# Attention with both heads in one instruction, and the queries' two parts stacked by transfers

## The chip, the cores and the metric

The kernel runs on one NeuronCore of a Trainium2 chip. The metric is the device time of one execution, in microseconds (us), taken over several runs. The core has five engines that run their own instruction streams in order: TensorE (PE; its weight loads are shown as PEld), VectorE (DVE), ScalarE (ACT), GpSimd (POOL) and SyncE (SP), which here only issues transfers. ACT issues some transfers too. Matmul results land in PSUM, which has eight banks of 512 fp32 values per partition; everything else is in SBUF or in the device memory.

## The reference, cut to what matters

One inference step of a two-layer decoder for 512 prompt positions and 8 sample positions, model width 1024. Layer 0 uses sliding-window attention (16 query heads, 2 key/value heads of width 64, window 128, one learned sink per head), layer 1 gated linear attention; each is followed by a gated convolutional FFN. The change is in layer 0's attention over the prompt:

```python
def sink_softmax(scores, mask, sink):
    s = jnp.where(mask, scores, NEG_INF)
    m = jnp.maximum(jnp.max(s, -1, keepdims=True), sink)
    p = jnp.exp(s - m)
    return p / (jnp.sum(p, -1, keepdims=True) + jnp.exp(sink - m))

def swa_prompt(x, w_qkv, b_qkv, sinks, w_o):
    q, k, v = qkv_proj(x, w_qkv, b_qkv, 0)          # with rotary positions
    ...                                             # blocks of 128, each with the block before it
    scores = jnp.einsum('bnqkgd,bnskd->bnkgqs', qb, kk) * ATTN_SCALE
    mask = (kpos >= 0) & (kpos <= qpos) & (qpos - kpos < WINDOW)
    probs = sink_softmax(scores, mask, sink)
    o = jnp.einsum('bnkgqs,bnskd->bnqkgd', probs, vv)
    return o @ w_o, ...
```

## The kernel before

**Units and groups.** The weights are cut into units of 128 output columns. The 520 positions are two groups: `a` has 256 prompt positions, `b` has 256 prompt and 8 sample positions. Each unit's function runs once for each group. Attention has ten units: one for the keys (`attn_k`), one for the values (`attn_v`) and eight for the queries (`attn_q`, c = 0 to 7); with two groups that is sixteen runs of `attn_q`. Unit c holds the query heads c and c + 8, one for each key/value head, stacked on partitions 0 to 63 and 64 to 127. "Both heads" below are these two, v = 0 and v = 1.

**Split numbers.** Products are made with rounded fp32 operands (fp32r). To keep fp32 accuracy each operand is a high part (a rounded copy) and a low part (the rest): `wh` and `wl` for weights (lines 156 to 161), `xh` and `xl` for activations; a product (lines 173 to 175) is three matmuls for each of eight blocks. For the scores, a query's high part is on 64 partitions and its low part on the other 64, so that one matmul with the stacked tile `qs` against `khi` and one against `klo` make all needed terms (lines 440 and 441).

**One run of `attn_q`** goes through four steps, with the next unit's product between them: (1) the product, its bias and scale on ACT (`ra`, line 362), the rotation (`rope`: a shuffle into `rb` on DVE, line 364; multiplications on POOL, line 365, and DVE, line 366; the sum `rr` on POOL, line 368), and the parts `qs` (ACT copy on line 414, DVE subtraction on line 415, once for each head, as the two heads' rows go to different partitions); (2) the scores into the PSUM tiles `sc`, one bank for each head, and for each head the masks (lines 450, 451 for group a, line 453 for group b), the sink as one more column (454), the negated maximum into `small` (455), two exponentials with their sums on ACT (457), the reciprocals (458) and the scaling of `pr` (POOL on line 463 for the first head, DVE on line 460 for the second); (3) transposes (469), a copy (471) and two triangular selections `pl` and `pu` on POOL (475); (4) the products with the values (488) and the split of the result into `hh`/`hl` or `hs` (198, 199).

**Buffers.** `sc` has two buffers in a PSUM pool that layer norm, the samples' attention and the gated linear attention use too; `tp` and `pv` have one bank each, the products four (`accp`). In SBUF `ra`, `rb`, `rr` and `qs` have two buffers each, `pr` four; the values before their transposition have one tile of their own, `vt` (line 393, read by the transposes on lines 397 and 402 and by a transfer on line 400).

**Order.** Tile's planner orders each engine's instructions along a simulated timeline, from the order in which the program makes them; buffers' releases and all semaphores come from it. Two functions of the program, `spawn` and `due`, put a unit's later steps behind the products that follow.

Of the kernel before, what the change touches and what calls it, by code (L numbers as in the profile page):

```python
# [20 lines left out]
P = 128  # L21
# [4 lines left out]
NT = SEQ + NS  # L26
# [42 lines left out]
C_SINK = C_LNB + 4 * KD  # L69
# [14 lines left out]
class Group:  # L84
    def __init__(self, i):
        self.i = i
        self.n = 256 if i == 0 else 256 + NS
        self.c0 = 256 * i
        self.name = "ab"[i]


class Net:
    def __init__(self, tc, ctx, I, O):
        self.tc, self.nc, self.I, self.O = tc, tc.nc, I, O
        self.groups = [Group(0), Group(1)]
# [12 lines left out]
        self.par = c.tile([P, NPAR], F32, name="par")  # L108
        self.ident = c.tile([P, P], F32, name="ident")
        self.ones_a = c.tile([P, P], F32, name="ones_a")  # L110
        nc.gpsimd.memset(self.ones_a, 1.0 / D)
        self.eps = c.tile([P, 2], F32, name="eps")
        nc.gpsimd.memset(self.eps[:, 0:1], NORM_EPS)
        nc.gpsimd.memset(self.eps[:, 1:2], 1.0)
        for i, g in enumerate(self.groups):
            s = [P, KD, g.n]
            g.x = self.act.tile(s, F32, name=f"x_{g.name}")


# [12 lines left out]
            g.hl = self.act.tile(s, F32R, name=f"hl_{g.name}")  # L132
        self.units = []
        self.w = {}

# [253 lines left out]
    def attn_v(self, g, u):  # L389
        nc, n = self.nc, g.n  # L390
        ps = self.product(g, u, g.xh, g.xl)
        vt = self.ap.tile([P, NT - 256], F32, name="vt", bufs=1)[:, :n]
        nc.scalar.activation(vt, ps, AF.Identity, bias=self.par[:, C_BQKV + 1:C_BQKV + 2])
        yield 1
        mp = self.mtile("tp")
        for b in range(2):
            nc.tensor.transpose(mp[:, b * P:(b + 1) * P], vt[:, b * P:(b + 1) * P], self.ident)
        nc.vector.tensor_copy(self.vtok[:, 2 * g.i:2 * g.i + 2, :], mp[:, :256].rearrange("p (b f) -> p b f", b=2))
        if g.i:
            nc.scalar.dma_start(out=self.O["v_prompt"], in_=vt[:, 128:256])  # L400
            mp = self.mtile("tp")
            nc.tensor.transpose(mp[:NS, :P], vt[:, 256:], self.ident)
            self.vs = self.ap.tile([NS, P], F32, name="vs")
            nc.vector.tensor_copy(self.vs, mp[:NS, :P])

    def attn_q(self, g, u, c):
        nc = self.nc
        ps = self.product(g, u, g.xh, g.xl)
        r = self.rope(g, ps, 0.125, self.bq[:, c:c + 1])
        qs = self.ap.tile([P, 2, 256], F32R, name="qs", bufs=2)  # L410
        for v in range(2):
            own = slice(64 * v, 64 * v + 64)
            oth = slice(64 - 64 * v, 128 - 64 * v)
            nc.scalar.activation(qs[own, v], r[own, :256], AF.Copy)
            nc.vector.tensor_tensor(qs[oth, v], r[own, :256], qs[own, v].bitcast(F32), op=ALU.subtract)  # L415
            if g.i:
# [14 lines left out]


        parts = []
        scs = [self.mtile("sc").rearrange("p (b k) -> p b k", b=2) for v in range(2)]
        for v in range(2):
            for b in range(2):
                n = 2 * g.i + b
                keys = slice(0, 256) if n == 0 else slice(P * (n - 1), P * (n + 1))
                qb = qs[:, v, b * P:(b + 1) * P]
                nc.tensor.matmul(scs[v][:, b], qb, self.khi[v][:, keys], start=True, stop=False)  # L440
                nc.tensor.matmul(scs[v][:, b], qb, self.klo[v][:, keys], start=False, stop=True)
        prs = []
        for v in range(2):
            h = c + 8 * v
            sc = scs[v]
            pr = self.ap.tile([P, 2, P + 2], F32, name="pr", bufs=4)
            small = self.ap.tile([P, 4], F32, name="small", bufs=4)
            nm, den = small[:, 0:2], small[:, 2:4]
            if g.i == 0:
                nc.vector.copy_predicated(sc[:, 0, 0:P], self.mask0.bitcast(I32), self.mask0)  # L450
                nc.vector.copy_predicated(sc[:, 1, 0:P], self.own[:, 0], sc[:, 1, P:])
            else:
                nc.vector.copy_predicated(sc[:, :, 0:P], self.own, sc[:, :, P:])
            nc.vector.tensor_copy(sc[:, :, P], self.par[:, C_SINK + h:C_SINK + h + 1].broadcast_to([P, 2]))
            nc.vector.tensor_reduce(nm, sc[:, :, 0:P + 1], axis=AX.X, op=ALU.max, negate=True)
            for b in range(2):
                nc.scalar.activation(pr[:, b, 0:P + 1], sc[:, b, 0:P + 1], AF.Exp, bias=nm[:, b:b + 1], accum_out=den[:, b:b + 1])
            nc.vector.reciprocal(den, den)
            if v:
                nc.vector.tensor_tensor(pr[:, :, 0:P], pr[:, :, 0:P], den.unsqueeze(2).broadcast_to([P, 2, P]), op=ALU.mult)  # L460
            else:
                for b in range(2):
                    nc.gpsimd.tensor_scalar(pr[:, b, 0:P], pr[:, b, 0:P], den[:, b:b + 1], 1.0, op0=ALU.mult, op1=ALU.mult)
            prs.append(pr)
        yield 1
        for pr in prs:
            tp = self.mtile("tp")[:, :256]
# [14 lines left out]
        for b in range(2):  # L482
            n = 2 * g.i + b
# [614 lines left out]
```

## Time and profile before

| | |
|---|---|
| median of 3 runs | 1159.49 us (1157.88 to 1160.13) |
| profiled execution | 1154.76 us |
| its span in the profile | 1153.0 us |
| mean granted TensorE clock | 0.992 |
| busy over the span | PE 96%, PEld 91%, DVE 70%, ACT 49%, POOL 30% |
| attention over the prompt | about the first 150 us |

The profile is of one execution. The span runs from its first to its last instruction; the time of the execution is 1.8 us longer. "Busy" is the time in which an engine has at least one instruction under way. Matmuls are pipelined, so a busy PE need not be at its peak. A row of the groups names the line, the engine, the operation, output and inputs, and then the busy time in us and the mean duration of one in ns, and the idle time of the engine just before them with what ended it. `<-` between two instructions in the list of waits reads "waited for".

### The profile page before, as it was taken

Reading aid. Unit: us, or ns where it says so; the run is one execution under the profiler, and the core shown is the slowest. Engines: PE = TensorE matmul, PEld = TensorE weight load, DVE = VectorE, ACT = ScalarE, POOL = GpSimd, SP = SyncE. Lnnn points to the kernel's source line nnn. Section 1 sums busy time; section 2 is a strip of 40 time slices with the busy share of each in tenths; the row PEclk is TensorE's granted clock in tenths of the full one; section 3 lists DMA queues with packets and bytes.
Section 4 is the critical chain, followed back from the end, with each engine's and each line's share of the span. In section 5 each row is a group of like instructions: output and inputs, shape, how many; then the busy total and the mean of one; then the engine's idle time right before and its main releaser. Section 6 shows DMA issues by size and latency. Waiting matters only on the chain.

```text
span 1153.0 us, 22833 instructions
## 1 busy us (share of the span) xinstructions
PE 1102.3 (96%) x8806; PEld 1052.4 (91%) x8806; DVE 809.6 (70%) x1679; ACT 565.2 (49%) x1228; POOL 348.0 (30%) x597
## 2 busy tenths in 40 slices
PE   7889988999999999999899999999999999999995
PEld 6788888999999999998899999898999999999994
DVE  7988869755665556568877688799756665566666
ACT  4466646633554245445545555457533553245433
POOL 5677768310011001056500100378100110010344
PEclk9999989999999999999999999999999999999998
DMA  6322022223232332243124454442323323233222
GB/s 221 129 78 88 2 76 97 83 83 119 102 109 93 97 106 92 92 132 110 38 92 126 132 185 145 153 136 68 110 91 115 106 92 110 92 103 100 74 63 75
DMA packets 48669, 118.62 MB, mean 103 GB/s; under 512 B 5768, under 2 KB 22192, under 8 KB 48560
## 3 DMA queue, kind: packets, MB, share of 16 engines
q1 hardware_dynamic: 46544, 115.41, 31.0%
q10 hardware_dynamic: 2016, 1.75, 0.5%
q8 instruction: 69, 1.13, 0.4%
q14 instruction: 40, 0.33, 0.1%
HBM read 108.67 MB, written 8.47 MB: 102 GB/s over the span
## 4 chain that ended last, share of the span: by engine, by line
PE 74%; DVE 14%; POOL 4%; issue 3%; DMA 2%; ACT 2%; SPq 0%; ACTq 0%; DVEq 0%; POOLq 0%
PE accp L174 15%; PE accp L191 15%; PE accp L175 15%; PE accp L173 15%; PE accp L192 8%; DVE wl L161 2%; DMA vb<-dv 1%; POOL x_b L298 1%; DVE qs L415 1%; POOL x_a L298 1%; DVE u L296 1%; PE pv L488 1%; DVE msq L276 1%; PE sc L761 1%; DVE rb L366 1%
## 5 line engine op out<-in xcount | busy, mean ns | idle before, releaser
L161 DVE TENSOR_TENSOR wl<-raw,wh 128x1024 fp32r<-128x1024 f32 (+2 forms) x189 | 230.5, 1221 | 107.4 <-ACT wh L158 103.3
L158 ACT ACTIVATE wh<-raw 128x1024 fp32r<-128x1024 f32 (+1 forms) x176 | 183.0, 1040 | 209.4 <-PE accp L174 196.9
L173 PE MATMUL accp<-xh_b,wh 128*128 128x264 f32 x976 | 271.6, 279 | 2.4 <-DVE hprod L594 2.4
L174 PE MATMUL accp<-xl_b,wh 128*128 128x264 f32 x976 | 271.3, 278 | 0.2
L175 PE MATMUL accp<-xh_b,wl 128*128 128x264 f32 x976 | 270.6, 277 | 0.0
L191 PE MATMUL accp<-xs_a,wh 128*128 128x512 f32 x576 | 196.3, 382 | 0.0
L173 PEld LDWEIGHTS accp<-xh_b,wh 128*128 128x128 f32 x976 | 184.9, 190 | 3.3 <-DVE hprod L594 2.8
L174 PEld LDWEIGHTS accp<-xl_b,wh 128*128 128x128 f32 x976 | 184.8, 189 | 3.1 <-DVE xl_b L301 0.6
L175 PEld LDWEIGHTS accp<-xh_b,wl 128*128 128x128 f32 x976 | 184.7, 189 | 0.6 <-issue 0.4
L192 PE MATMUL accp<-xs_a,wl 128*128 128x256 f32 x576 | 145.4, 273 | 0.0
L173 PE MATMUL accp<-hh_b,wh 128*128 128x264 f32 x480 | 134.2, 280 | 3.2 <-ACT hh_b L198 3.2
L174 PE MATMUL accp<-hl_b,wh 128*128 128x264 f32 x480 | 134.5, 280 | 0.0
L175 PE MATMUL accp<-hh_b,wl 128*128 128x264 f32 x480 | 133.6, 278 | 0.0
L191 PEld LDWEIGHTS accp<-xs_a,wh 128*128 128x128 f32 x576 | 109.2, 190 | 11.3
L173 PE MATMUL accp<-xs_a,wh 128*128 128x256 f32 x400 | 111.4, 284 | 5.7 <-DVE x_b L219 2.1
L174 PE MATMUL accp<-xs_a,wh 128*128 128x256 f32 x400 | 111.4, 281 | 3.4 <-DVE xs_a L301 2.7
L175 PE MATMUL accp<-xs_a,wl 128*128 128x256 f32 x400 | 111.1, 280 | 3.0 <-DVE wl L161 3.0
L192 PEld LDWEIGHTS accp<-xs_a,wl 128*128 128x128 f32 x576 | 110.3, 191 | 1.9
L173 PEld LDWEIGHTS accp<-hh_b,wh 128*128 128x128 f32 x480 | 91.7, 191 | 3.6 <-ACT hh_b L198 3.5
L202 POOL COPY hist<-aext 128x2 f32<-128x2 f32 x44 | 8.9, 202 | 284.7 <-DVE aext L572 281.6
L174 PEld LDWEIGHTS accp<-hl_b,wh 128*128 128x128 f32 x480 | 91.6, 191 | 1.4 <-issue 0.3
L175 PEld LDWEIGHTS accp<-hh_b,wl 128*128 128x128 f32 x480 | 91.5, 191 | 0.2
(320 smaller groups left out, 2522.1 us busy)
## 6 DMA issues: line engine op xcount, KB each, us to landing
raw<-in_w_up SPq DMA_DIRECT2D x88, 512.0 KB, 3.4
raw<-in_w_down SPq DMA_DIRECT2D x32, 512.0 KB, 3.4
raw<-in_w_gla SPq DMA_DIRECT2D x24, 512.0 KB, 3.4
raw<-in_w_mix_o SPq DMA_DIRECT2D x16, 512.0 KB, 3.5
raw<-in_w_down SPq DMA_DIRECT2D x16, 384.0 KB, 2.9
sgla<-in_state_gla SPq DMA_DIRECT2D x16, 256.0 KB, 3.1
vb<-dv SPq DMA_DIRECT2D x16, 256.0 KB, 4.0
out_gla_s<-sgla SPq DMA_DIRECT2D x16, 256.0 KB, 2.7
```

The costliest lines, as they stand in the source:

```text
L158: nc.scalar.activation(h[:, c], r[:, c], AF.Copy)
L161: nc.vector.tensor_tensor(l[:, c], r[:, c], h[:, c].bitcast(F32), op=ALU.subtract)
L173: nc.tensor.matmul(o, h[:, ks], xh, start=k == 0, stop=False)
L174: nc.tensor.matmul(o, h[:, ks], xl, start=False, stop=False)
L175: nc.tensor.matmul(o, l[:, ks], xh, start=False, stop=k == nt - 1)
L191: both = lambda: nc.tensor.matmul(o, h[:, ks], in_turn(rs[:, k].rearrange("p t q j -> p t (q j)")), start=k == 0, stop=last)
L192: low = lambda: nc.tensor.matmul(o[:, :P], l[:, ks], in_turn(rh[:, k]), start=False, stop=False)
L276: nc.vector.scalar_tensor_tensor(q, q, 0.5, nv, op0=ALU.mult, op1=ALU.mult)
L296: nc.vector.tensor_tensor(u, x[:, m], r, op=ALU.mult)
L298: ts = nc.gpsimd.tensor_scalar(x[:, m], u, sc(m), bi(m), op0=ALU.mult, op1=ALU.add)
L366: nc.vector.tensor_tensor(b, b, tab[:, 1], op=ALU.mult)
L415: nc.vector.tensor_tensor(qs[oth, v], r[own, :256], qs[own, v].bitcast(F32), op=ALU.subtract)
```

## The change

It does five things, all in layer 0's attention over the prompt but the second:

- **Parts of the queries.** The high part of both heads is made by one ACT copy and the low part by one DVE subtraction, both on 128 partitions, into a new tile `hl` (two buffers). Four transfers, issued by ACT, then put the four blocks of 64 partitions and 256 columns in their places in `qs`.
- **`sc` is one tile** of two banks for the whole program. `attn_q` uses both halves; every other user gets one half, in turn.
- **Masks, sinks, maxima, reciprocals.** One instruction works on both heads' banks where there was one for each head. Masks and sinks come from broadcast access patterns. The exponentials stay four, one for each head and block.
- **Scaling.** The scaling of both heads comes behind the reciprocals of both.
- **`vt` becomes a buffer of the tag `ra`**, which has two.

```diff
+        self.sc2, self.sc_i = self.mps.tile([P, 2, 512], F32, name="sc"), 0
...
     def mtile(self, tag):
-        return self.mps.tile([P, 512], F32, name=tag, bufs=2 if tag == "sc" else 1)
+        if tag == "sc":
+            self.sc_i += 1
+            return self.sc2[:, self.sc_i % 2]
+        return self.mps.tile([P, 512], F32, name=tag)
...
-        vt = self.ap.tile([P, NT - 256], F32, name="vt", bufs=1)[:, :n]
+        vt = self.ap.tile([P, NT - 256], F32, name="ra", bufs=2)[:, :n]
...
+        hl = self.ap.tile([P, 2, 256], F32R, name="hl", bufs=2)
+        nc.scalar.activation(hl[:, 0], r[:, :256], AF.Copy)
+        nc.vector.tensor_tensor(hl[:, 1], r[:, :256], hl[:, 0].bitcast(F32), op=ALU.subtract)
         qs = self.ap.tile([P, 2, 256], F32R, name="qs", bufs=2)
-        for v in range(2):
-            own = slice(64 * v, 64 * v + 64)
-            oth = slice(64 - 64 * v, 128 - 64 * v)
-            nc.scalar.activation(qs[own, v], r[own, :256], AF.Copy)
-            nc.vector.tensor_tensor(qs[oth, v], r[own, :256], qs[own, v].bitcast(F32), op=ALU.subtract)
+        for part in range(2):
+            for v in range(2):
+                nc.scalar.dma_start(out=qs[64 * part:64 * part + 64, v].bitcast(F32),
+                                    in_=hl[64 * v:64 * v + 64, part].bitcast(F32))
...
-        scs = [self.mtile("sc").rearrange("p (b k) -> p b k", b=2) for v in range(2)]
+        sc = self.sc2.rearrange("p v (b k) -> p v b k", b=2)
...
+        small = self.ap.tile([P, 2, 4], F32, name="small", bufs=4)
+        nm, den = small[:, :, 0:2], small[:, :, 2:4]
+        if g.i == 0:
+            nc.vector.copy_predicated(sc[:, :, 0, 0:P], self.mask0.bitcast(I32).unsqueeze(1).broadcast_to([P, 2, P]),
+                                      self.mask0.unsqueeze(1).broadcast_to([P, 2, P]))
+            nc.vector.copy_predicated(sc[:, :, 1, 0:P], self.own, sc[:, :, 1, P:])
+        else:
+            own = self.own[:, 0:1].unsqueeze(1).broadcast_to([P, 2, 2, P])
+            nc.vector.copy_predicated(sc[:, :, :, 0:P], own, sc[:, :, :, P:])
+        sink = self.par[:, C_SINK + c:C_SINK + c + 9:8]
+        nc.vector.tensor_copy(sc[:, :, :, P], sink.unsqueeze(2).broadcast_to([P, 2, 2]))
+        nc.vector.tensor_reduce(nm, sc[:, :, :, 0:P + 1], axis=AX.X, op=ALU.max, negate=True)
         for v in range(2):
...
             for b in range(2):
+                nc.scalar.activation(pr[:, b, 0:P + 1], sc[:, v, b, 0:P + 1], AF.Exp, bias=nm[:, v, b:b + 1], accum_out=den[:, v, b:b + 1])
             prs.append(pr)
+        nc.vector.reciprocal(den, den)
+        for b in range(2):
+            nc.gpsimd.tensor_scalar(prs[0][:, b, 0:P], prs[0][:, b, 0:P], den[:, 0, b:b + 1], 1.0, op0=ALU.mult, op1=ALU.mult)
+        nc.vector.tensor_tensor(prs[1][:, :, 0:P], prs[1][:, :, 0:P], den[:, 1].unsqueeze(2).broadcast_to([P, 2, P]), op=ALU.mult)
```

More of the change, by code (lines that the diff above doesn't have):

```diff
@@ L409, in attn_q @@
         r = self.rope(g, ps, 0.125, self.bq[:, c:c + 1])
+        hl = self.ap.tile([P, 2, 256], F32R, name="hl", bufs=2)
+        nc.scalar.activation(hl[:, 0], r[:, :256], AF.Copy)
+        nc.vector.tensor_tensor(hl[:, 1], r[:, :256], hl[:, 0].bitcast(F32), op=ALU.subtract)
         qs = self.ap.tile([P, 2, 256], F32R, name="qs", bufs=2)
-        for v in range(2):
-            own = slice(64 * v, 64 * v + 64)
-            oth = slice(64 - 64 * v, 128 - 64 * v)
-            nc.scalar.activation(qs[own, v], r[own, :256], AF.Copy)
-            nc.vector.tensor_tensor(qs[oth, v], r[own, :256], qs[own, v].bitcast(F32), op=ALU.subtract)
-            if g.i:
+        for part in range(2):
+            for v in range(2):
+                nc.scalar.dma_start(out=qs[64 * part:64 * part + 64, v].bitcast(F32),
+                                    in_=hl[64 * v:64 * v + 64, part].bitcast(F32))
+        if g.i:
+            for v in range(2):
+                own = slice(64 * v, 64 * v + 64)
                 o = c + 8 * v
@@ L439, in attn_q @@
                 qb = qs[:, v, b * P:(b + 1) * P]
-                nc.tensor.matmul(scs[v][:, b], qb, self.khi[v][:, keys], start=True, stop=False)
-                nc.tensor.matmul(scs[v][:, b], qb, self.klo[v][:, keys], start=False, stop=True)
+                nc.tensor.matmul(sc[:, v, b], qb, self.khi[v][:, keys], start=True, stop=False)
+                nc.tensor.matmul(sc[:, v, b], qb, self.klo[v][:, keys], start=False, stop=True)
         prs = []
+        small = self.ap.tile([P, 2, 4], F32, name="small", bufs=4)
@@ L449, in attn_q @@
[L449 to L455, printed above, removed]
```

11 lines of the change are left out of this document (removed).

## The prediction

> **What bounds the kernel now.** I read the page's engine shares and its chain first, then the windows of the attention, then that stretch's chain in order of time, its groups by shape, and its waits.
>
> ```profile
> PE 74%; DVE 14%; POOL 4%; issue 3%; DMA 2%; ACT 2%; SPq 0%; ACTq 0%; DVEq 0%; POOLq 0%
> ```
>
> Over the whole span PE carries the chain, but DVE's 14% are not spread evenly. The windows (length, then busy us and instructions of PE, PEld, DVE, ACT, POOL, the granted clock, DMA) show where they lie; the last row is a stretch behind the attention in which PE never waits.
>
> ```profile
> 24.00:124.00 100.00, 87.30 (x773) 80.04 (x772) 90.78 (x243) 58.30 (x198) 76.17 (x131) 1.00 0.27 87
> 24.00:140.00 116.00, 102.49 (x921) 93.17 (x920) 102.25 (x282) 68.04 (x239) 84.88 (x152) 1.00 0.23 75
> 160.00:180.00 20.00, 20.00 (x177) 19.90 (x175) 17.17 (x29) 10.47 (x18) 11.52 (x11) 1.00 0.33 107
> ```
>
> From 24 to 140 us, where the sixteen queries' runs lie, DVE is busy 102.25 of 116 us (88%). PE shows 102.49, but with its modelled ends: it issues 921 matmuls. Behind the attention it issues 177 in 20 us, 0.113 us each. So PE is not full here, DVE is. A piece of the chain in order of time (start, us, what) says the same: one DVE instruction behind another.
>
> ```profile
> 47.21 0.87 DVE qs L415
> 48.10 0.43 DVE rb L366
> 48.56 0.43 DVE qs L415
> 49.54 0.37 DVE small L455
> ```
>
> ```profile
> ACT pr L457 <- DVE small L455: 23.8, 18, 3.5
> PEld sc L440 <- ACT pr L457: 8.8, 11, 2.8
> ```
>
> ACT's exponentials wait 23.8 us for DVE's maxima, and PE's scores wait for the exponentials to free a bank. What is taken off DVE here is worth time, until another engine is as full.
>
> **DVE's part, step by step.** The rows by shape (busy us, mean ns):
>
> ```profile
> L415 DVE TENSOR_TENSOR qs<-rr,qs 64x256 fp32r<-64x256 f32 x32 | 18.7, 585 | 1.0
> L199 DVE TENSOR_TENSOR xs_a<-x_a,xs_a 128x256 fp32r<-128x256 f32 x8 | 4.0, 545 | 1.3 <-ACT xs_a L198 1.3
> L450 DVE COPY_PREDICATED sc<-mask 128x128 f32<-128x128 int32 x16 | 6.2, 385 | 1.7 <-PE sc L441 1.6
> L451 DVE COPY_PREDICATED sc<-own,sc 128x128 f32<-128x128 int32 x16 | 4.6, 285 | 0.1
> L453 DVE COPY_PREDICATED sc<-own,sc 128x256 f32<-128x256 int32 x16 | 6.8, 422 | 0.9 <-PE sc L441 0.7
> L727 DVE COPY_PREDICATED attm<-causal,sc 128x256 f32<-128x256 int32 x8 | 3.5, 441 | 1.9 <-PE sc L724 1.9
> L454 DVE COPY sc<-par 128x2 f32<-128x2 f32 x32 | 5.0, 158 | 0.4
> L455 DVE TENSOR_REDUCE small<-sc 128x2 f32<-128x258 f32 x32 | 13.5, 421 | 0.8
> L505 DVE TENSOR_REDUCE small<-sc 128x1 f32<-128x128 f32 x1 | 0.3, 292 | 1.0 <-POOL pu L475 1.0
> L458 DVE RECIPROCAL small<-small 128x2 f32<-128x2 f32 x32 | 5.1, 158 | 4.5 <-ACT pr L457 4.3
> ```
>
> - Low parts: 32 x 0.585 = 18.7 become 16 on 128 partitions at 0.545 (line 199, the same subtraction from SBUF) = 8.7: 10.0 us less.
> - Group a's masks: 6.2 + 4.6 = 10.8. From 128 to 256 columns costs 422 - 285 = 137 ns, so 8 x (0.385 + 0.137) + 8 x 0.422 = 7.6: 3.2 less.
> - Group b's masks: 6.8 become 8 x (0.422 + 2 x 0.137) = 5.6: 1.2 less. The broadcast mask of line 727 costs 441 against 422, so the new patterns should cost almost nothing; 512 columns over two banks are not in the trace.
> - Sinks and reciprocals: 16 fewer of each at 0.158, 5.1 less.
> - Maxima: from 128 to 258 columns 292 to 421, 1 ns a column, so 516 columns take 0.68; 13.5 become 10.9: 2.6 less.
>
> Together 22.1 us. The short ones partly overlap their neighbours in DVE's pipeline; with half of those 5.1 us it is 19.6. I take 20: DVE 82 of 116 us.
>
> **How much of it reaches the end.** At the same 88% DVE would need 82 / 0.88 = 93 us. PE's floor, with the products with the values at the pitch of this row ((0.44 - 0.27) / 3 = 0.056, one matmul showing 0.27):
>
> ```profile
> 60.68 0.44 PE L488 MATMUL pv<-pu,vtok 128*64 128x128 f32 x4
> ```
>
> Line 488 issues 208 of the 921 here, so 208 x 0.056 + 713 x 0.113 = 92 us. POOL keeps its work: 84.88 / 0.88 = 96.5, which is 19.5 below 116. So 19 us is the most I expect from this part, and POOL is late next.
>
> **What the change adds.** ACT's queue:
>
> ```profile
> L414 ACT ACTIVATE qs<-rr 64x256 fp32r<-64x256 f32 x32 | 13.3, 414 | 7.8 <-POOL rr L368 6.4 <-PE sc L441 1.0
> ```
>
> ```profile
> 34.44 0.42 ACT L379 ACTIVATE khi<-rr 64x256 fp32r<-64x256 f32 x1 [2.89 <-POOL rr L368]
> 34.45 0.38 ACTq L387 DMA_DIRECT2D out_k_prompt<-rr  x1
> ...
> 42.41 0.47 ACT L393 ACTIVATE vt<-accp,par 128x264 f32<-128x264 f32 x1
> 42.91 0.34 ACTq L400 DMA_DIRECT2D out_v_prompt<-vt  x1
> 43.30 0.47 ACT L362 ACTIVATE ra<-accp,bq 128x256 f32<-128x256 f32 x1 [0.41 <-ACT vt L393]
> ```
>
> Sixteen copies go (13.3 / 2 = 6.7 us less), 64 issues come at 0.36 each: 23 us, and ACT's 68.04 become 84.4. An issue runs beside the ACTIVATE ahead of it (at 34.45 it is hidden entirely), unless it needs that one's result (at 42.91: 0.41 us of idle ACT). Ends: all hidden, 6.7 us less; none hidden, 16.3 more. I take half of them hidden, 11.5 - 6.7 = 5 more, and 3 more because the two issues of the low parts wait in ACT's queue for DVE's subtraction, 0.2 us a query, with exponentials and `pt` copies behind them that PE and POOL wait for. Together 8 us given back.
>
> The landing: qs is ready when its last transfer is in. The second head's is the fourth issue, the first head's the third, 1.1 us after the first.
>
> ```profile
> out_gla_p<-sp ACTq DMA_DIRECT2D x4, 128.0 KB, 1.7
> ...
> ident<-in_ident SPq DMA_DIRECT2D x1, 64.0 KB, 3.3
> ```
>
> Neither goes from SBUF to SBUF. With 1.7 us (ACT's queue, from SBUF) the first head waits 2.8 us, with 3.3 (the loaded start) 4.4. The gap between the end of line 415 and the first scores covers it; the shortest and the last of the gaps are in these rows, with the first scores of all:
>
> ```profile
> 29.72 0.28 PE L440 MATMUL sc<-khi,qs 128*128 128x256 f32 x1
> ...
> 117.40 0.42 DVE L415 TENSOR_TENSOR qs<-rr,qs 64x256 fp32r<-64x256 f32 x1
> ...
> 120.18 0.39 PE L440 MATMUL sc<-khi,qs 128*128 128x256 f32 x1
> ...
> 124.15 0.87 DVE L415 TENSOR_TENSOR qs<-rr,qs 64x256 fp32r<-64x256 f32 x2
> ...
> 133.26 0.36 PE L440 MATMUL sc<-khi,qs 128*128 128x256 f32 x1
> ```
>
> Behind the first query, the gaps run from 120.18 - 117.82 = 2.4 to 133.26 - 125.02 = 8.2 us. Spread evenly, about five of fifteen are below 4.4, by 1 us each: ends 0.4 (one gap, 2.8 - 2.4) and 5; I take 1, the ACT row being nearest. The Trainium skill, "DMA: Bandwidth & Descriptors", section "Anatomy of one DMA", gives a transfer about 2.0 us of fixed cost and the rest by its bytes; by that (estimate: 1.1 + 2.0 + 0.15 for 64 KB = 3.3) the shortest gap would miss by 0.9 us instead of 0.4.
>
> `vt` in `ra`: it is written at 42.41 and last read by line 402.
>
> ```profile
> L402 PE MATMUL tp<-ident,vt x1: 273/273/273, 72.4 to 72.4; 128*8 128x128 f32 x1
> ```
>
> ```profile
> 59.15 0.51 ACT L362 ACTIVATE ra<-accp,bq 128x264 f32<-128x264 f32 x1
> ```
>
> ```profile
> 65.87 0.74 POOL L368 TENSOR_TENSOR rr<-ra,rb 128x264 f32<-128x264 f32 x1
> ```
>
> For these 30 us the queries have one `ra` left, whose life is 66.61 - 59.15 = 7.5 us, against one query each (133.26 - 29.72) / 15 = 6.9 us: 0.6 x 4.4 queries = 2.6 at most, none if the life shrinks with DVE's queue. I take 1. The first head's scaling starts two exponentials later, about 0.7 us; the product between steps (2) and (3) covers it, and without that cover it is 11 us. `sc` as one tile of two banks keeps the count of banks; I cost it at nothing outside attention.
>
> **Sum.** -19 + 8 + 1 + 1 = -9 us. The profiled execution took 1154.76, 4.73 below the median, so 1145.8 there, and 1150.5 us in the median.
>
> **The rivals.**
>
> *All of it arrives.* ACT's issues are hidden behind its ACTIVATEs. For it: ACT idles 48 of the 116 us now. Against it: an issue behind its own source is exposed. -14 to -20 us: 1140 to 1145.
>
> *ACT takes DVE's place.* All issues are exposed (+16.3 instead of +5), with the 3 us and the two small terms: -19 + 16.3 + 3 + 2 = +2, about 1161.5: no change that a measurement can tell. For it: the row at 42.91. Against: three quarters of ACT's time would still be enough, 84.4 of 116.
>
> *Slower: one loop through both banks.* Now each head has its own bank, and its own loop of scores, mask, maximum and exponentials; the two go in turn. Then both go round together: scores 0.6 us, masks up to 0.95, sink 0.16, maximum 0.68, four exponentials 4 x 0.37 and the last sum 0.2, about 4.1 us with nobody in the way. A query has 6.9 us now, so 2.8 us of queueing decide: a weight split on DVE ahead of the masks (1.35),
>
> ```profile
> L161 DVE TENSOR_TENSOR wl<-raw,wh 128x1024 fp32r<-128x1024 f32 x13 | 17.6, 1351 | 1.6 <-POOL wh L160 1.3 <-ACT wh L158 0.3
> ```
>
> four issues on ACT ahead of the exponentials (1.4) and part of a product on PE ahead of the scores (24 x 0.113 = 2.7) come to 5.4 when they all meet. At 3.2 on average it is 0.4 x 16 = +6 us: 1165. For it: PE's scores wait for exponentials already. Against: 13 weight splits in 150 us are less than one a query.
>
> *Transfers one behind the other.* Should the four not overlap, the last lands 4 x 1.7 = 6.8 us after the first issue; eleven of the fifteen gaps would then be short, by 2.2 us on average: 25 us, -9 + 25 = +16, 1175. The Trainium skill's page "DMA: Bandwidth & Descriptors" says in "Rules for kernel authors" that transfers to disjoint partition halves serialise, since they share the same engines, and that one transfer on 128 partitions is better. Against it:
>
> ```profile
> 0.00:20.00 20.00, 15.82 (x93) 13.15 (x93) 13.11 (x26) 8.79 (x21) 9.10 (x19) 1.00 0.84 266
> ```
>
> 266 GB/s at the start, where one 128 KB transfer in 1.7 us alone is 77: transfers overlap well. I give it 0.03. No trace before has halves issued together.
>
> **How the numbers follow.** Forecast (part of the gain, 1143 to 1157): 0.50. All of it: 0.12. ACT bound, no change: 0.14. Slower, by the loop (0.17) or by late landings and `ra` at their upper ends (0.04) or by serial transfers (0.03): 0.24. Within 0.2%, 2.3 us, a measurement can't tell it from no change; the three runs span that much. So faster 0.62, same 0.14, slower 0.24. The upper ends together, -19 + 19.3 + 5 + 2.6, give +8 and 1167; the range 1142 to 1164 leaves out a tenth on each side.
>
> **What would show it.** Right: DVE's busy time in the attention near 82 us, lines 450 to 458 at half the count with 0.4 to 0.7 us each; the waits of the exponentials for the maxima far below 23.8 us; ACT over 80 us with its issues; the same work behind the attention starting some 9 us earlier. Wrong: ACT's idle time gone or ended by DVE's subtraction; score matmuls waiting for transfers or, longer than now, for exponentials; line 362 waiting for line 368 while `vt` is alive. A planner that reorders the seam at the attention's end could also hide or add a few us.

## The result: 1176.4 us, slower by 1.4%

| | before | after |
|---|---|---|
| median | 1159.81 us (1157.88 to 1160.18) | 1176.41 us (1173.67 to 1178.98) |
| ratio to before, 95% interval | | 1.0139 (1.0118 to 1.0160) |
| profiled execution | 1154.76 us | 1178.98 us |

Both medians are of four executions. Before's profile is 5.0 us below its median and after's 2.6 above, so the two profiles lie 24.2 us apart where the medians lie 16.6 apart. The experiments below share out the 16.6 (by the ratio, 0.0139 x 1160, it is 16.1). One execution of e8 took 2307.52 us, about twice the others, and is left out of its row.

The relief of DVE came about as forecast. In the attention, 24 to 140 us, the same row as before's (length, busy us and count of PE, PEld, DVE, ACT, POOL, granted clock, DMA):

```profile
24.00:140.00 116.00, 101.02 (x895) 92.68 (x893) 85.53 (x186) 56.38 (x209) 84.16 (x143) 0.97 0.40 112
```

DVE fell from 102.25 to 85.53 us, and yet PE got less done in it, 895 matmuls for 921. The groups by shape show the expected half counts at about the expected durations (the broadcast mask of line 457 is the longest miss, 612 ns for 522), with one idle time that was not there (the last figure: idle just before, and what ended it):

```profile
L465 DVE TENSOR_REDUCE small<-sc 128x4 f32<-128x516 f32 x16 | 11.1, 695 | 0.6
...
L419 DVE TENSOR_TENSOR hl<-rr,hl 128x256 fp32r<-128x256 f32 x16 | 8.5, 532 | 1.9 <-ACT hl L418 1.5 <-POOL pr L473 0.3
...
L462 DVE COPY_PREDICATED sc<-own,sc 128x512 f32<-128x512 int32 x8 | 5.5, 692 | 3.9 <-PE sc L452 3.9
...
L457 DVE COPY_PREDICATED sc<-mask 128x256 f32<-128x256 int32 x8 | 4.9, 612 | 0.1
...
L459 DVE COPY_PREDICATED sc<-own,sc 128x256 f32<-128x256 int32 x8 | 3.4, 427 | 0.2
...
L471 DVE RECIPROCAL small<-small 128x4 f32<-128x4 f32 x16 | 2.8, 173 | 13.8 <-ACT pr L469 13.8
...
L464 DVE COPY sc<-par 128x4 f32<-128x4 f32 x16 | 2.6, 164 | 0.4
```

After's list of waits up to 150 us says the same from both sides. The exponentials wait for maxima 12.3 us where it was 23.8; in return DVE waits for the exponentials, 13.8:

```profile
DVE small L471 <- ACT pr L469: 13.8, 10, 2.2
...
ACT pr L469 <- DVE small L465: 12.3, 7, 3.7
```

The timeline of after shows why, in one query's round (start, us, engine, line; scores on 451, mask on 462, sinks on 464, maxima on 465, exponentials on 469):

```profile
101.99 0.39 PE L451 MATMUL sc<-khi,qs 128*128 128x256 f32 x1 [0.25 <-ACT pr L469]
...
103.24 0.69 DVE L462 COPY_PREDICATED sc<-own,sc 128x512 f32<-128x512 int32 x1 [0.16 <-PE sc L452]
...
105.28 0.70 DVE L465 TENSOR_REDUCE small<-sc 128x4 f32<-128x516 f32 x1
...
106.01 0.37 ACT L469 ACTIVATE pr<-sc,small 128x129 f32<-128x129 f32 x1 [2.81 <-DVE small L465]
...
107.31 0.21 ACT L469 ACTIVATION_READ_ACCUMULATOR pr<-sc,small 128x1 f32 x1
...
107.57 0.38 PE L451 MATMUL sc<-khi,qs 128*128 128x256 f32 x1 [1.12 <-ACT pr L469]
```

All eight score matmuls of a query follow the last exponential of the one before, here by 0.05 us (107.57 - 107.52); in nine of the fifteen rounds they follow within 0.5 us. Nothing of the next query is on the common tile while this one is. PE's own waits for the exponentials do not show the loss: its scores wait 4.3 us where it was 6.4, and the weight loads ahead of them 5.4 where it was 8.8.

The page's chain has changed little in its shares:

```profile
PE 71%; DVE 13%; POOL 5%; issue 4%; DMA 4%; ACT 2%; ACTq 0%; SPq 0%; DVEq 0%; POOLq 0%
```

DMA went from 2 to 4%: landings of `qs` lie on it now. That is no loss by itself, since without the transfers after is slower (e4 below).

Two more rows date the rest: the first FFN's first copy into `aext`, and the last update of the state `sgla`, near the end of the gated linear attention (GLA). First before, then after (durations as minimum, median and maximum in ns, then first and last start):

```profile
L568 ACT COPY aext<-accp x88: 350/368/379, 194.0 to 1098.7; 128x256 f32<-128x256 f32 x44, 128x264 f32<-128x264 f32 x44
...
L839 DVE SCALAR_TENSOR_TENSOR sgla<-vb,kraw,sgla x32: 472/480/972, 622.6 to 757.4; 128x256 f32<-128x256 f32 x32
```

```profile
L578 ACT COPY aext<-accp x88: 345/367/379, 201.5 to 1122.9; 128x256 f32<-128x256 f32 x44, 128x264 f32<-128x264 f32 x44
...
L849 DVE SCALAR_TENSOR_TENSOR sgla<-vb,kraw,sgla x32: 472/480/966, 634.1 to 783.2; 128x256 f32<-128x256 f32 x32
```

The first FFN begins 7.5 us later (201.5 - 194.0). From there to the last state update it is 581.7 us instead of 563.4: another 18.3 us are lost in a part that the change's list of five things hardly touches. (Before's 563.4 is the shortest of nine such kernels in the table below; against the middle one of them, 567.5, it is 14 us.) Only the second of them, `sc` as one tile for the whole program, reaches it.

### The profile page after: what moved, and what is told of

Read it like the earlier page. It is cut to its first block, busy times and chain, and to the rows that moved or that the text cites. A ratio compares the mean times of both kernels' runs of the same rounds, so it can differ in the third digit from the quotient of the medians.

```text
span 1177.2 us, 22871 instructions
## 1 busy us (share of the span) xinstructions
PE 1114.4 (95%) x8806; PEld 1062.1 (90%) x8806; DVE 796.8 (68%) x1591; ACT 560.2 (48%) x1212; POOL 349.8 (30%) x597
## 4 chain that ended last, share of the span: by engine, by line
PE 71%; DVE 13%; POOL 5%; issue 4%; DMA 4%; ACT 2%; ACTq 0%; SPq 0%; DVEq 0%; POOLq 0%
PE accp L193 15%; PE accp L176 14%; PE accp L175 14%; PE accp L177 14%; PE accp L194 7%; DVE wl L163 2%; DMA vb<-dv 2%; DMA qs<-hl 1%; POOL x_b L303 1%; POOL x_a L303 1%; DVE u L301 1%; PE pv L498 1%; DVE sgla L849 1%; DVE msq L281 1%; ACT pr L469 1%
## 5 line engine op out<-in xcount | busy, mean ns | idle before, releaser
L175 PE MATMUL accp<-xs_a,wh 128*128 128x256 f32 x400 | 113.2, 288 | 6.3 <-DVE x_b L222 1.1
L176 PE MATMUL accp<-xs_a,wh 128*128 128x256 f32 x400 | 113.0, 285 | 4.1 <-DVE xs_a L306 3.4
```

The source lines that it names most:

```text
L175: nc.tensor.matmul(o, h[:, ks], xh, start=k == 0, stop=False)
L176: nc.tensor.matmul(o, h[:, ks], xl, start=False, stop=False)
```

## The experiments

Each row: median, ratio to before (1160 us) with its 95% interval, and from its profile the first `aext` copy and the time from it to the last state update. "Pair" is a tile of two banks. e11 to e14 and e16 also have `vt` in `ra`, and e11 and e13 have no transfers.

| run | what | median | ratio (interval) | first FFN | to end of GLA |
|---|---|---|---|---|---|
| before | | 1159.81 | 1 | 194.0 | 563.4 |
| after | | 1176.41 | 1.0139 (1.0118 to 1.0160) | 201.5 | 581.7 |
| e1 | before, `sc` one pair | 1204.82 | 1.0380 (1.0364 to 1.0395) | 228.0 | 582.4 |
| e7 | before, two tiles in turn | 1160.45 | 0.9994 (0.9981 to 1.0008) | 195.4 | 567.0 |
| e15 | before, one pair behind attention | 1174.12 | 1.0121 (1.0099 to 1.0144) | 196.0 | 582.0 |
| e2 | after, one pair in attention only | 1164.79 | 1.0042 (1.0029 to 1.0055) | 198.3 | 567.9 |
| e4 | after without transfers | 1182.09 | 1.0190 (1.0169 to 1.0212) | 201.6 | 581.6 |
| e5 | e4, one pair in attention only | 1169.67 | 1.0076 (1.0055 to 1.0096) | 202.8 | 568.1 |
| e6 | before, `vt` in `ra` | 1162.91 | 1.0015 (1.0002 to 1.0029) | 196.9 | 565.4 |
| e3 | e6 with transfers | 1157.33 | 0.9968 (0.9954 to 0.9982) | 193.1 | 567.5 |
| e9 | transfers, `vt` on its own | 1162.34 | 1.0014 (1.0002 to 1.0027) | 198.1 | 567.5 |
| e10 | e3, issued by SP | 1154.88 | 0.9955 (0.9939 to 0.9972) | 190.4 | 568.7 |
| e8 | before without low parts | 1147.23 (three executions) | 0.9891 (0.9863 to 0.9919) | 183.2 | 568.6 |
| e11 | joint masks, two pairs, 2 product banks | 1219.04 | 1.0507 (1.0490 to 1.0523) | 192.0 | 616.1 |
| e12 | four banks, 2 product banks | 1216.52 | 1.0489 (1.0470 to 1.0509) | 196.1 | 611.7 |
| e13 | e11's banks in attention only | 1164.27 | 1.0036 (1.0016 to 1.0057) | 191.4 | 574.9 |
| e16 | e12's banks in attention only | 1166.46 | 1.0060 (1.0038 to 1.0081) | 194.2 | 574.3 |
| e14 | e13 with SP's transfers | 1163.40 | 1.0026 (1.0012 to 1.0040) | 190.9 | 575.0 |

### Is it the common tile? (e1, e7, e15)

e1 is before with the pair alone; masks stay one for each head.

```diff
+        self.sc2, self.sc_i = self.mps.tile([P, 2, 512], F32, name="sc"), 0
...
+        if tag == "sc":
+            self.sc_i += 1
+            return self.sc2[:, self.sc_i % 2]
...
-        scs = [self.mtile("sc").rearrange("p (b k) -> p b k", b=2) for v in range(2)]
+        scs = [self.sc2[:, v].rearrange("p (b k) -> p b k", b=2) for v in range(2)]
```

> Only the score tile is changed: one tile of two banks for the whole program, halves given to its users in turn; in the attention each head keeps its half and its own instructions. Theory A (the one tile costs time in the gated linear attention, where its users no longer take whichever bank is free): slower than before by 9 to 17 us, with the first gate copy of the first FFN within 3 us of before's 194.0 us and the loss between 560 and 790 us. Rival B (any change to the attention only moves the planner's order behind it, the tile itself costs nothing): within 4 us of before.

It is 44 us slower (0.038 x 1160): 34 us later at the first FFN, and with 582.4 us from there to the end of GLA. Theory A had only the second part, 9 to 17 us; that the pair costs far more inside attention, with masks for each head, it missed. e1's timeline shows the mechanism (masks on line 454, exponentials on 461):

```profile
61.76 0.20 ACT L461 ACTIVATION_READ_ACCUMULATOR pr<-sc,small 128x1 f32 x1
...
62.07 0.28 DVE L454 COPY_PREDICATED sc<-mask 128x128 f32<-128x128 int32 x1
...
64.49 0.20 ACT L461 ACTIVATION_READ_ACCUMULATOR pr<-sc,small 128x1 f32 x1
...
64.86 0.29 PE L444 MATMUL sc<-khi,qs 128*128 128x256 f32 x1
```

The mask at 62.07 is the second head's. It touches the other bank, and its scores had long been in; it starts 0.11 us after the first head's last exponential (61.96). A reciprocal that needs that exponential stands ahead of it on DVE, at 61.99, so this one place does not decide which of the two held it back. The next query's scores, both heads', start after the last exponential of the second head (64.69). Over the whole attention it is the same: of e1's 112 masks, sinks and maxima on `sc` none overlaps an exponential, and of its 128 score matmuls none overlaps an exponential or one of those 112. Instructions of different engines on different halves of the tile run one after another, as if they used the same bank.

That could also have come from the fixed turn of the two halves. e7 keeps the turn and makes the halves two tiles:

```diff
...
+        self.scs2, self.sc_i = [self.mps.tile([P, 512], F32, name=f"sc{i}") for i in range(2)], 0
...
+            return self.scs2[self.sc_i % 2]
```

> The kernel before with its two score buffers as two separate tiles for the whole program, given to the users in a fixed turn, each head of the attention its own: the order of users is that of the run with one tile (which took 1205 us), only that the two banks are two tiles. Theory A1 (two banks of one tile are not used by two engines at once, because instructions on one tile are put in order by the whole tile): as before, 1157 to 1165 us, scores of the second head and exponentials of the first beside each other again. Theory A2 (the fixed turn costs, not the common tile): 10 to 45 us slower than before.

It takes before's time (0.9994). In its timeline the second head's mask runs between the first head's exponentials:

```profile
66.62 0.37 ACT L461 ACTIVATE pr<-sc,small 128x129 f32<-128x129 f32 x1 [0.87 <-DVE small L459]
...
66.85 0.64 DVE L454 COPY_PREDICATED sc<-mask 128x128 f32<-128x128 int32 x1
...
66.89 0.19 ACT L461 ACTIVATION_READ_ACCUMULATOR pr<-sc,small 128x1 f32 x1
```

In e7 25 of the 112 overlap an exponential, and of the 128 score matmuls 26 overlap an exponential and 51 a mask, sink or maximum; in before it is 26, 30 and 49. So what costs is one tile over both banks, not the turn and not the banks: e1 and e7 use the same two banks in the same turn. The semaphores behind it are made by the planner, which orders uses of a tile; whether the chip itself would want them can't be told from these runs.

e15 leaves attention as it was; where it ends, its pool of two single banks is closed and the pair opened:

```diff
...
+        self.close(self.sc_cm)
+        self.sc_pool = self.stack.enter_context(self.tc.tile_pool(name="sctwo", bufs=1, space=PSUM))
+        self.sc2 = self.sc_pool.tile([P, 2, 512], F32, name="sc")
```

> Before, with `sc` in two tiles of one bank until attention ends and then in one tile of two banks whose halves are used in turn. Theory (the common tile costs outside attention what the profiles of three kernels show between the first FFN and the end of the gated linear attention, 581.6 to 582.4 us against 563.4 to 568.7 with two tiles): 11 to 16 us slower than before, 1171 to 1176. Rival (that stretch is long because attention handed over late, not because of the tile): within 4 us of before, 1158 to 1164.

14 us slower (0.0121 x 1160), all between the first FFN and the end of GLA: 582.0 us there, as in after, e1 and e4 (581.6 to 582.4), against 563.4 to 568.7 in the nine kernels, before among them, that have two tiles there and the products' four banks in one pool. The theory held: that loss is no echo of a late attention. Nor is it the closing and opening of a pool, which e2 and e5 do too (567.9 and 568.1 us), or the fixed turn, which e7 has (567.0). Two waits of GLA show it, in before, then in after (the copy `vk` waits for transposes, the decay `dmn` for its product in `sc`; before's list has no `dmn` row for this above 0.9 us):

```profile
ACT vk L748 <- PE tp L746: 3.2, 3, 1.8
```

```profile
ACT vk L758 <- PE tp L756: 13.2, 8, 4.6
...
DVE dmn L689 <- PE sc L685: 9.9, 4, 3.4
```

e15 has them too, 13.3 and 9.6 us. At GLA's end the layer norm's first sums go through `sc` as well; before they stand at 734.2 us, after at 758.1:

```profile
L223 PE MATMUL sc<-x_a,ones_a x2: 379/379/379, 734.2 to 734.4; 128*128 128x256 f32 x2
```

```profile
L228 PE MATMUL sc<-x_a,ones_a x2: 379/380/382, 758.1 to 758.3; 128*128 128x256 f32 x2
```

Which of `sc`'s users there costs most was not taken apart.

### After, with the pair in attention only (e2)

```diff
...
         self.close(self.ap_cm)
+        self.sc2 = None
+        self.close(self.sc_cm)
+        self.sc_cm = self.tc.tile_pool(name="sctwo", bufs=2, space=PSUM)
+        self.sc_pool = self.stack.enter_context(self.sc_cm)
```

> The changed kernel, but its one score tile lives only until the attention ends; then two separate buffers take its banks again. Theory A: the loss of the gated linear attention goes, the 7.5 us lost up to the first FFN stay: 1165 to 1169 us. Rival B: no better than the changed kernel, 1174 to 1179 us.

1.0042 instead of 1.0139: the pair behind attention costs 11 us of after's 16 (0.0139 x 1160), and 4.9 remain. The stretch to the end of GLA is 567.9 again.

### The change without its transfers, and its transfers alone (e3 to e6, e9, e10)

e4 is after with before's two copies and two subtractions for `qs`; e5 is e4 with e2's edit.

> The changed kernel with the queries' parts made as before, head by head and without transfers; masks, sinks, maxima and reciprocals for both heads at once, one score tile. Theory C: first gate copy 0 to 6 us earlier than before's 194.0; with the loss of the gated linear attention by theory A the total is 1163 to 1172. Rival D: first gate copy 5 to 10 us later than before, total 1174 to 1182.

> The changed kernel without the transfers (the queries' parts head by head as before) and with the score tile given back to two buffers when the attention ends; so what is left of the change is the joint masks, sinks, maxima and reciprocals on one tile, inside the attention. Theory D (the common tile and its one loop cost the attention its time, the transfers nothing): first gate copy 3 to 8 us later than before's 194.0, total 1163 to 1171. Rival C (the transfers cost it): first gate copy within 2 us of before or earlier, total 1154 to 1161.

Without transfers after is slower still, by 5.9 us (1.0190 - 1.0139), and e5 by 3.9 than e2: theory C, that the transfers cost the time, falls, and D, the loop, holds. e6 and e3 separate the last two parts:

```diff
-        vt = self.ap.tile([P, NT - 256], F32, name="vt", bufs=1)[:, :n]
+        vt = self.ap.tile([P, NT - 256], F32, name="ra", bufs=2)[:, :n]
```

> The kernel before with the values' tile in the rotation's two buffers and nothing else changed. By the prediction's term it costs 0 to 2.6 us; the transfers alone (which hold this too) came 3.3 us below before. If the tile is the hidden cost of that run: 1162 to 1164; if it is free: within 2 us of before.

> The kernel before with the queries' parts made for both heads and stacked by the four transfers (and the values' tile sharing the rotation's buffers, without which they don't fit); masks, sinks, maxima for each head alone, score buffers as before. Theory C (the transfers, through 64 issues of 0.5 us on ScalarE and their landing, cost the attention its time): first gate copy 5 to 10 us later than before's 194.0, total 1165 to 1170. Rival D (the common loop of both heads through both banks costs it): the transfers alone save 10 us of VectorE and the first gate copy comes 2 to 8 us earlier, total 1152 to 1158.

`vt` in `ra` costs 1.7 us (0.0015 x 1160). With the transfers on top it is 0.9968, so they win 5.5 us. After's rows on them (issues on ACT's queue in ns, then us from issue to landing):

```profile
L423 ACTq DMA_DIRECT2D qs<-hl x64: 468/514/782, 27.3 to 128.2; - x64
...
DMA to landing us min/median/max: 1.9/2.1/6.1
```

An issue takes 0.51 us of ACT's queue, not 0.36, together 33 us. What these 33 us cost, e10 asks, by issuing from SP:

```diff
-                nc.scalar.dma_start(out=qs[64 * part:64 * part + 64, v].bitcast(F32),
+                nc.sync.dma_start(out=qs[64 * part:64 * part + 64, v].bitcast(F32),
```

> The run with the transfers alone (two `sc` tiles, masks per head, `vt` in `ra`), but the 64 transfers are issued by SP instead of ACT. On ACT they occupied 64 x 0.51 = 33 us of its queue. Theory (part of these 33 us is on the path, as the prediction's +8 for ACT had it): 2 to 6 us faster than with ACT's issues, 1151 to 1156. Rival 1 (ACT has slack enough and hides its issues): the same as with ACT's issues within 1.5 us, 1156 to 1160. Rival 2 (SP's transfers of weights, which wait for their buffers, stand ahead of the queries' on SP): the first scores of each query are late and it is slower than before, 1165 or more.

0.9955 against e3's 0.9968: 1.5 us, and the intervals overlap. The theory's 2 to 6 us is not shown, though e10's 1154.88 lies in its 1151 to 1156; ACT hid most of its 33 us. Rival 2 fell: e10's first FFN starts 2.7 us earlier than e3's. e10 is the fastest kernel here that computes all, 4.9 us below its own before (1159.76).

> Before with the queries' two parts made for both heads in `hl` and stacked by the four transfers, but `vt` in a tile of its own as before, and `hl` with one buffer instead of two to find the room; masks and the two `sc` tiles as before. Theory (the transfers are a gain and `vt` in `ra` costs 2.5 us of it): the run with both was 3.2 us faster than before, so this one is 5 to 6 us faster, 1153 to 1157. Rival (the next query's copy into the single `hl` waits for the last transfer out of it, or the cost of `vt` in `ra` was within the measurement's scatter): not faster than the run with `vt` in `ra`, 1157 or more.

e9 missed: 1.0014, the rival's outcome, but the wait that it named does not show it. Rows of e3, then of e9:

```profile
L412 DVE TENSOR_TENSOR hl<-rr,hl 128x256 fp32r<-128x256 f32 x16 | 8.5, 532 | 2.7 <-ACT hl L411 2.6
...
L411 ACT ACTIVATE hl<-rr 128x256 fp32r<-128x256 f32 x16 | 6.7, 419 | 16.6 <-POOL rr L368 11.7 <-DMA qs<-hl 4.9
```

```profile
L412 DVE TENSOR_TENSOR hl<-rr,hl 128x256 fp32r<-128x256 f32 x16 | 11.1, 695 | 0.6 <-ACT hl L411 0.6
...
L411 ACT ACTIVATE hl<-rr 128x256 fp32r<-128x256 f32 x16 | 6.8, 424 | 6.5 <-DMA qs<-hl 3.7 <-POOL rr L368 2.5 <-issue 0.3
```

With one `hl` the copy waits for transfers 3.7 us, less than the 4.9 with two; the same subtraction takes 695 ns on average for 532, and the granted clock from 24 to 140 us is 0.96 for 1.00. Why is open, and so the transfers' gain of 5.5 us is shown only with two buffers for `hl` and `vt` in `ra`.

### Joint instructions with a second pair (e11 to e14, e16)

If a missing second buffer is the fault, two pairs should mend it. There are eight banks; e11 takes them from the products (two banks for four), and e12 is its control.

```diff
-ACCS = 4
+ACCS = 2
...
+        sc = self.mps.tile([P, 2, 512], F32, name="sc", bufs=2).rearrange("p v (b k) -> p v b k", b=2)
```

> Masks, sinks, maxima and reciprocals for both heads at once, as in the change, without its transfers and with `vt` in `ra`; but `sc` is two tiles of two banks each (two pairs), for which the products keep two banks instead of four. To be compared with the run of four single banks for `sc` and two for the products, masks per head. Theory (the loss in attention is that a pair on one tile leaves no second buffer, the joint instructions themselves save DVE's time): within 3 us of that run or faster, by up to 5 us. Rival (joint instructions cost by themselves, because both heads' scores must be in before the first mask and the exponentials come in a block): slower than that run by 5 us or more, as with one pair.

> Before with `vt` in `ra`, four single-bank buffers for `sc` instead of two, and two for the products instead of four: the run that the one with two pairs is compared with. Both theories: two banks fewer for the products cost something in all stages (a product's bank is freed only when ACT has copied it out), two more for the scores win some in attention; I expect 1155 to 1185. It is here only for its difference to the run with two pairs.

Both lie far above the 1155 to 1185 given for e12: with two product banks the whole program takes 57 us longer (0.0489 x 1160). Within the pair the rival falls (e11 is 2 us behind e12, not 5 or more), and up to the first FFN e11 is 4.1 us ahead. e13 and e16 confine the exchange to attention, at whose end `sc` has two single banks again and the products get two more from a second pool, and e14 adds SP's transfers to e13:

```diff
+    def acctile(self):
+        self.acc_i += 1
+        pool = self.acc if self.acc2 is None or self.acc_i % 2 else self.acc2
+        return pool.tile([P, 512], F32, name="accp")
...
+        self.close(self.sc_cm)
+        self.sc_pool = self.stack.enter_context(self.tc.tile_pool(name="sctwo", bufs=2, space=PSUM))
+        self.acc2 = self.stack.enter_context(self.tc.tile_pool(name="acctwo", bufs=2, space=PSUM))
```

> Masks, sinks, maxima and reciprocals for both heads at once with two tiles of two banks for `sc` (two pairs), but only in attention, where the products have two banks; when attention ends `sc` has two single banks and the products four again. No transfers, `vt` in `ra`. Compared with the run of four single banks in attention. Theory (the joint instructions gain once a second pair exists; with two pairs in the whole program the first FFN began at 192.0 us against 196.1 with four single banks): 3 to 6 us faster than that run, 1154 to 1159. Rival (the joint instructions gain nothing by themselves, the 4.1 us were scatter of single profiles): within 2 us of that run or slower.

> Before with `vt` in `ra` and, in attention only, four single banks for `sc` and two for the products; two and four behind it. It is the run that the one with two pairs in attention is compared with. Both theories: with four banks in the whole program the first FFN began at 196.1 us against 196.9 with two, so about the time of the run with `vt` in `ra` alone, 1158 to 1164.

> The run with two pairs in attention, and the queries' two parts stacked by transfers that SP issues: both of the change's savings on DVE without its common tile. Theory (what DVE is spared adds up; the transfers on SP gave 5 us, or 7 against the run with `vt` in `ra` alone): 4 to 8 us faster than the run with two pairs alone and the fastest so far, 1147 to 1154. Rival (with the masks' relief DVE is no longer what attention waits for, so the second saving passes on nothing): within 2 us of the better of its two parts, 1154 to 1158.

e13 is 2.8 us faster than e16 (1.0036 against 1.0060; the intervals overlap), between the theory's 3 to 6 and the rival's 2, as in the first FFN's start (191.4 against 194.2). With a second pair the joint instructions cost nothing that shows, and may win a little. In microseconds both missed, e13 (1164.27) the theory's 1154 to 1159 and e16 its 1158 to 1164: behind attention all three kernels with the products' banks in two pools need 574 to 575 us to GLA's end, some 7 more than with one pool.

e14 is no faster than e13 within the noise (1.0026 against 1.0036; the intervals overlap): the second saving passes on nothing that shows, as its rival had it. Both ranges given for e14, up to 1158, were missed: neither had the 7 us behind attention. DVE is relieved once more, and attention waits elsewhere (e14's window, and a row of its waits):

```profile
24.00:140.00 116.00, 105.80 (x940) 96.65 (x938) 91.86 (x206) 61.50 (x227) 93.17 (x159) 0.99 0.39 111
```

```profile
ACT hl L426 <- POOL rr L381: 19.8, 10, 3.7
```

DVE has 91.86 us to e13's 101.20, but now POOL is busier than DVE, 93.17 us, and the queries' copy waits 19.8 us for POOL's rotation (17.1 in e13).

### What DVE's time is worth (e8)

e8 leaves out the low parts of the queries, line 415; `qs` is two fixed tiles, set to zero once, and all matmuls stay.

> The kernel before without the low parts of the queries: the 32 subtractions of line 415 (18.7 us of VectorE) are left out, and the rows of the stacked tile for them stay zero. Nothing is added. Theory E (VectorE is the bound of the attention, and what is taken off it passes to the end): first gate copy 8 to 16 us earlier than before's 194.0, total 1144 to 1152. Rival F (the other engines' queues are as full, so that little passes): first gate copy 0 to 4 us earlier, total 1155 to 1160.

12.6 us come of 18.7 us of DVE's work (0.0109 x 1160; by the interval 9.4 to 15.9): about two thirds pass on. The subtraction was also a step on each query's way to its scores; how much of the 12.6 is that, and not DVE's time, was not taken apart.

## Why the prediction was wrong

The step that failed is the last sentence of its part on what the change adds: "`sc` as one tile of two banks keeps the count of banks; I cost it at nothing outside attention." It counted banks and not tiles. Outside attention the pair costs 14 us alone (e15) and 11 in after (e2). No rival held it, and without it after would have been e2's 1164.8.

Inside attention the likeliest case was the wrong one too. **The rival "one loop through both banks"** is what the profile shows, and its 1165 is what e2, the change with its pair in attention only, took. Its sizes were less right than its sum. The round with nobody in the way was put at 4.1 us. The shortest of the sixteen, from the first score to the end of the last exponential's sum, takes 4.53 (136.46 - 131.93):

```profile
131.93 0.28 PE L451 MATMUL sc<-khi,qs 128*128 128x256 f32 x1
...
132.75 0.28 PE L452 MATMUL sc<-klo,qs 128*128 128x256 f32 x1
...
136.24 0.22 ACT L469 ACTIVATION_READ_ACCUMULATOR pr<-sc,small 128x1 f32 x1
```

The eight scores alone last 1.10 us of it (133.03 - 131.93) where 0.6 stood; eight at the prediction's own 0.113 would have made 0.9. The first fifteen rounds take 6.0 us in the mean, and 1.1 us pass between one round and the next, so the mean distance of queries, from the first to the sixteenth one's first score matmul, went from 6.9 us to (139.93 - 33.24) / 15 = 7.1, where the rival had 4.1 + 3.2 = 7.3. That is only half of what the queries lost: the sixteenth's scores start 6.7 us later than before's (139.93 for 133.26), and 3.5 of these the first query has already (33.24 for 29.72), which the rival did not have. That its 1165 came out so near is partly luck. That weight splits are rare was no argument against it: five of the sixteen rounds take over 7 us, and in each of the three that start at 70.69, 80.45 and 88.95 us splits of 1.2 to 1.8 us stand on DVE between the scores and the maximum.

By terms, each measured one uncertain by 2 to 3 us, from the intervals of its two runs; the last row follows one chain of runs (before, e6, e3, e2, after), whose steps add up by construction:

| term | predicted | measured | from |
|---|---|---|---|
| joint masks, sinks, maxima (about half of the -19) | -9.5 | +8.6, +7.1 on one pair; -2.8 on two | e2 to e3, e5 to e6; e13 to e16 |
| queries' parts: DVE -9.5, ACT +8, landing +1 | -0.5 | -5.5, -5.9, -3.9 | e3 to e6; after to e4; e2 to e5 |
| `vt` in `ra` | +1 | +1.7 | e6 |
| one tile outside attention | 0 | +11.2, +13.2, +14.0 | after to e2; e4 to e5; e15 |
| sum | -9 | 1.7 - 5.5 + 8.6 + 11.2 = +16 | |

- **DVE's relief** was sized rightly: of 59.9 us in the seven groups the seven rows above keep 38.8, so 21.1 went where 22.1 was worked out. That 19 of 20 us reach the end was too generous even without the loop: e8 passes on 12.6 of 18.7.
- **ACT.** The issues were underpriced (0.51 us for 0.36) and their effect overpriced: the transfers' part wins 4 to 6 us where ACT's +8 was to take back nearly all that DVE won.
- **Landing.** 2.1 us in the median (6.1 at most) lies between the two ends taken, 1.7 and 3.3. The Trainium skill's "DMA: Bandwidth & Descriptors" (section "Anatomy of one DMA") has about 2.0 us fixed, but for transfers that GpSimd issues and not ACT; the trace's 2.1 agrees with that number. The prediction's term missed the first query: its scores start at 32.3 us in e3 and 33.24 in after for 29.72 before and 28.8 in e4, which has no transfers, as nothing covers a first transfer.
- **Transfers one behind the other** fell: issued some 0.5 us apart, they land 2.1 us after their issue in the median. The Trainium skill's rule that transfers to disjoint halves serialise ("Rules for kernel authors" of the same page) is not tested by this: no run here issues the four together.
- **"POOL is late next"** was right, where the loop doesn't stand in the way: e14.

The chance of slower was 0.24, and the range's 1164 fell short by 12 us, about the price of the pair outside attention. The range did not fit its own chances either: it was to leave out a tenth on each side, but the rival with 0.17 had its middle at 1165, above it.

## What to carry to other kernels

Count tiles, not only banks or bytes: when buffers of a rotating tag are merged into one tile, ask for every user of the tag, in the whole program, which engine worked on one part while another worked on the other, and price the loss of that overlap as you would a buffer less. An instruction that serves two buffers at once needs a second pair of them, and its saving has to be set against what the pair's banks were doing elsewhere. Time taken off an engine that was 88% busy was worth about two thirds of itself here, and a second such saving nothing, once the next engine was as full.

## What the runs showed of the hardware

- An issue of a transfer from SBUF to SBUF held ACT's queue 0.47 to 0.78 us in after (up to 1.59 in e3), where two issues to device memory in before show 0.34 and 0.38.
- A short pause of PE was followed by half its clock, as here in after's GLA (start, us; the first rows are of the timeline, the last one of the windows, its granted clock 0.51):

```profile
737.43 0.28 PE L177 MATMUL accp<-hs_a,wl 128*128 128x256 f32 x1
...
739.67 0.50 PE L175 MATMUL accp<-hs_a,wh 128*128 128x256 f32 x1 [1.97 <-DVE gsmall L806]
...
742.53 0.42 PE L176 MATMUL accp<-hs_a,wh 128*128 128x256 f32 x1
...
742.74 0.42 PE L177 MATMUL accp<-hs_a,wl 128*128 128x256 f32 x1
...
743.16 0.27 PE L176 MATMUL accp<-hs_a,wh 128*128 128x256 f32 x1
```

```profile
739.70:743.00 3.30, 3.30 (x16) 3.30 (x17) 1.80 (x1) 1.04 (x3) 0.41 (x1) 0.51 0.72 220
```

  PE idles 1.97 us, and then its matmuls start 0.21 us apart for 3.3 us, before they are back at 0.11: the pause costs about 1.6 us more than itself. The Trainium skill's "TensorE: Matmul & The Clock Gate" (section "Part 1: The HAM clock gate") says that the clock is halved after an idle window of about 3.4 us and comes back after about as long; the way back agrees (3.3 us), the way down came here after a shorter pause. The length of a pause alone does not decide it: in before's attention PE idles 2.56 us, longer, up to 40.99 us, and the granted clock from 41 to 44 us is 1.00.
